# Recurrence of a hybrid trunk: keys of all batches projected first, front and inverse 0 beside the receptance projections, the value input mixed early and reread from DRAM

## The chip, the core and the metric

The program runs on one core of a Trainium2 chip. The core has a matrix engine (TensorE: PE, and PEld for its weight loads), a vector engine (VectorE, DVE), a scalar engine (ScalarE, ACT), a general engine (GpSimd, POOL), a synchronising engine that issues nearly all transfers (SyncE, SP), and 16 DMA engines. Tiles live in SBUF, matmul results in eight banks of PSUM. The metric is the device time of one execution in microseconds (us), as the median of several runs.

## The reference

Two layers over a sequence of 512 positions of width 1024, in fp32: layer 0 mixes tokens with an RWKV-7 recurrence, layer 1 with a chunked spatial gating unit, and a SwiGLU network (width 2816) follows each. The change touches only the recurrence:

```python
xx = _token_shift(x) - x
xs = x[None] + xx[None] * mix[:, None, None, :]
r, k, v = jnp.einsum('cbtd,cde->cbte', xs[:3], w_rkv)
w_raw = (w0 + jnp.tanh(xw @ w1) @ w2)
decay = jnp.exp(-jnp.exp(-softplus(-w_raw) - 0.5))
a = sigmoid(a0 + (xa @ a1) @ a2);  g = sigmoid(xg @ g1) @ g2
kk = normalised(k * k_k);  k = k * (1.0 + (a - 1.0) * k_a)
# per head, state S (64 x 64), t = 0..511:
#   S = S diag(decay_t) + (S (-kk_t)) (kk_t a_t)^T + v_t k_t^T ;  y_t = S r_t
y = groupnorm(y) * gn_w + gn_b + sum(r * k * r_k) * v
out = (y * g) @ w_o
```

Here `xs[0]`, `xs[1]` and `xs[2]` are the receptance, key and value inputs: each is the normed x and its shift by one position, mixed with its own coefficients.

## The kernel before

Every fp32 operand of a large matmul is split into a rounded part (hi, made by ACT) and a rest (lo, made by DVE), and three matmuls give the product (`mm3`). The kernel runs the recurrence, its output projection, network 0, the gating unit and network 1. The program is written in order into a tile framework; the pools give out slots by tag, and a planner at build time (`schedule_with_timeline_sim=True`) fixes each engine's order from a simulated course in which an instruction may pass earlier ones that are not ready or have no slot.

The 16 heads are handled in four batches of four heads. For each batch b:

- **P** (`kr_proj`, L654): the key and the receptance projection, each of two weights (`feat_proj`, L647): a weight of 512 KB is loaded by SP, split into whi and wlo (two buffers each, L182), and 24 matmuls of 512 columns go into one of two "pl" banks; ACT copies the result out (L660). The inputs are the mixed and split tiles xk and xr (`mixed_split`, L616): per tile ACT and DVE mix (L612, L613), then ACT and DVE split.
- **E** (`early`, L740): decay, its running sum and exponentials, key normalisation, bonus; it ends by storing four scaled arrays to DRAM (sa, sb: L811, L814).
- **F** (`front`, L824): loads them back (ST, L829; MV, L835), multiplies them chunk by chunk (lm, L851), and spreads the products into MV, BX and LA by ACT copies and POOL selections (L854 to L870).
- **B** (`back`, L873): inverts a unit triangular matrix per chunk: one DVE transposition (LX, L882), 15 dependent steps on DVE (L896, L898), two transpositions (L901, L902), chains of 32x32 matmuls on PE (Qp, Np, Tp, Q2p, T2p: L918 to L950) with copies into bdT, then products that close MV (mp, L959; gh, L966; L968, L969).
- **S** (`scan`, L971): eight dependent steps of small matmuls (us, L995; Yp, L1008) with the value rows reread from DRAM (L980), and the output Y.
- **N** (`finish`, L1077): group norm, bonus and gate, stored to DRAM (od) for the output projection; batch 3 is kept on chip in halves.

**X** mixes and splits the value input once for all batches, and **V** (`v_proj`, L698) projects the values of batch b (384 matmuls of 256 columns for all four, in two "pb" banks) and stores them to DRAM.

The order of the program is the list PLAN (L35): after the hidden layer of the gate and the mixing of xk come P0 (in which xr is mixed), E0, P1, E1, P2, E2, P3, E3, X0, F0, B0, F1, V0 to V3, B1, S0, F2, S1, F3, N0, B2, N1, B3, S2, N2, S3, N3. XV (L36) says in which pool each of the eight value tiles lies.

The slots matter to the change: "s" has 17 tiles of 4 KB a partition (h, half of xk, xr, part of the value input, MV, BX), "x" 4 (half of xk, part of the value input, then Y), "e2" 7 (k, r, Pp, ST, LA, LX and, later, split output weights), "e" 2 of half the size (xs, vev, ob), "f0", "gain" and "hn" 2 each, "bd" 1 (the tile tws of early 1 and 3, later bdT) and "hid" 1 (the hidden layer of decay, later Dt).

Of the kernel before, what the change touches and what calls it, by code (L numbers as in the profile page):

```python
# [13 lines left out]
P = 128  # L14
# [5 lines left out]
C = 64  # L20
# [11 lines left out]
BANKS_F1 = dict(tr=(1, 2), gu=(4, 0, 3, 5, 7, 6), R=(4, 0), Q=(3, 5), Z=(7, 6), h0=(1, 2, 0, 5), h1=(4, 3, 7, 6))  # L32
SLOTS = 17
E2 = 7
PLAN = "P0 E0 P1 E1 P2 E2 P3 E3 X0 F0 B0 F1 V0 V1 V2 V3 B1 S0 F2 S1 F3 N0 B2 N1 B3 S2 N2 S3 N3".split()  # L35
XV = "xxxessss"  # L36
XSLOTS = 13
LAG = 2
PLAIN = 2
# [91 lines left out]
class Trunk:  # L131
# [384 lines left out]
    def rwkv(self, x0):  # L516
# [3 lines left out]
        with ExitStack() as ctx:  # L520
# [4 lines left out]
            sa = [dp.tile([P, 2, NC, 2, C], F32, name="sa") for _ in range(4)]  # L525
            sb = [dp.tile([P, 2, NC, 2, C], F32, name="sb") for _ in range(4)]
            od = dp.tile([KT, P, T], F32, name="od")

            def e(name, shape=(P, T), dt=F32):
                return rp.tile(list(shape), dt, name=name, tag="e", bufs=2)  # L530
# [85 lines left out]
            def mixed_split(c, where):  # L616
# [6 lines left out]
                    r.append(s)  # L623
                return r

            wrkv = i["rwkv_w_rkv"][0]
            q2 = range(2)
            units = [(hh, q) for hh in range(2) for q in q2]
# [22 lines left out]
                    self.mm3(acc, (hi[:, kt, :], lo[:, kt, :]), (xs[kt][:, 0, :], xs[kt][:, 1, :]), kt == 0, kt == KT - 1)  # L651
                return acc

            def kr_proj(b):  # L654

                o = []
                for w, xs, n in ((wrkv[1], xk, "k"), (wrkv[0], xr, "r")):
                    t = e2(n)
                    for q in q2:
                        a.copy(t[:, q, :], feat_proj(w, xs, 2 * b + q))  # L660
                    o.append(t)
                return o

            sg = rp.tile([P, 2, T], F32R, name="sg")
            sgb = rp.tile([96, T], F32R, name="sgb")
# [74 lines left out]
            def early(b, k, r):  # L740
# [4 lines left out]
                fcs = lambda q: slice(q * P, (q + 1) * P)  # L745


                if b % 2:
                    tws = bd("tws", [P, 2, 2, T])
                    tw, ta = tws[:, 0], tws[:, 1]  # L750
                    room = lambda name: self.sm.tile([P, 2, T], F32, name=name, tag="hn", bufs=2)
                else:
                    tw, ta = (self.f0p.tile([P, 2, T], F32, name=n, tag="f0", bufs=2) for n in ("tw", "ta"))
                    room = lambda name: gslot(name, [P, 2, T])
# [69 lines left out]
            def front(b, o):  # L824

                MV, ST, BX = {}, {}, {}
                for hh in range(2):
                    st = ST[hh] = e2("ST", (P, 2, 4, 2, C))
                    nc.sync.dma_start(out=st.rearrange("p q c n t -> p q (c n t)"),  # L829
                                      in_=sb[b][:, :, 4 * hh:4 * hh + 4].rearrange("p q c n t -> p q (c n t)"))  # L830
                    for q in q2:
                        mv = MV[hh, q] = s4("MV", [P, 4, 2, 2, C])
                        for hd in range(2):
                            g.memset(mv[head[1 - hd], :, :, hd], 0.0)
                            nc.sync.dma_start(out=mv[head[hd], :, :, hd].rearrange("p c n t -> p (c n) t"),  # L835
                                              in_=sa[b][head[hd], q, 4 * hh:4 * hh + 4].rearrange("p c n t -> p (c n) t"))
                LA = e2("LA", (P, 2, NC, C))
                Dm = self.f0p.tile([P, 2, 528], F32, name="Dm", tag="f0", bufs=2)
                g.memset(full(Dm), 0.0)
                g.memset(Dm.rearrange("p b r -> p (b r)")[:, 0:1024:33], 1.0)  # L840
                for hh, q in units:
                    st, mv = ST[hh][:, q], MV[hh, q]

                    bx = BX[hh, q] = s4("BX", [P, 4, 4, C])
                    for hd in range(2):
                        g.tensor_copy(bx[head[hd], 2 + hd], self.ident[head[hd], head[hd]].unsqueeze(1).broadcast_to([64, 4, C]))
                    for hd in range(2):
                        rows, other = head[hd], head[1 - hd]
                        lm = self.bank("pl", "lm")
                        for cc in range(4):  # L850
                            mm(lm[:, cc * P:(cc + 1) * P], st[:, cc].rearrange("p n t -> p (n t)"), mv[:, cc, :, hd, :], start=True, stop=True)  # L851
                        lv = lm.rearrange("p (c a t) -> p c a t", c=4, a=2)
                        la = LA[:, q, 4 * hh:4 * hh + 4]
                        a.copy(mv[other, :, :, hd], lv[other])  # L854
                        for n in range(2):
                            upper(mv[other, :, n, hd], n - 1)
                        a.copy(la[rows], lv[rows, :, 0, :])
                        upper(la[rows], -1)
                        a.copy(bx[rows, 1], lv[rows, :, 1, :])
                        upper(bx[rows, 1], 0)  # L860

                    sf = st.rearrange("p c n t -> p c (n t)")
                    pt = self.bank("pl", "bkt")
                    for cc in range(4):
                        nc.tensor.transpose(pt[:, cc * P:(cc + 1) * P], sf[:, cc], self.ident)
                    pv = pt.rearrange("p (c h f) -> p c h f", c=4, h=2)
                    for hd in range(2):
                        rows, other = head[hd], head[1 - hd]
                        a.copy(bx[rows, 0], pv[rows, :, hd])
                        a.copy(bx[other, 2 + hd], pv[other, :, hd])  # L870
                o.update(MV=MV, BX=BX, LA=LA, Dm=Dm)

            def back(b, o):  # L873
# [18 lines left out]
                for j in range(15):  # L892
# [3 lines left out]
                    v.tensor_tensor(tv, LXd[:, :, j + 1:16, j:j + 1].broadcast_to([P, 2, n, j + 1]),  # L896
                                    Dmd[:, :, j:j + 1, 0:j + 1].broadcast_to([P, 2, n, j + 1]), op=ALU.mult)
                    v.tensor_tensor(Dmd[:, :, j + 1:16, 0:j + 1], Dmd[:, :, j + 1:16, 0:j + 1], tv, op=ALU.add)  # L898
                Dt = rp.tile([P, 16, 2, 32], F32, name="Dt", tag="hid", bufs=1)
                Dn = self.sm.tile([P, 16, 2, 32], F32, name="hn", tag="hn", bufs=2)  # L900
                v.transpose(Dn.rearrange("p u x s -> p s (u x)"), full(Dm).rearrange("p t s -> p s t"))  # L901
                v.transpose(Dt.rearrange("p u x t -> p t (u x)"), full(Dm))  # L902
# [68 lines left out]
            def scan(b, o, then=None):  # L971

                MV, pc = o["MV"], o["pc"]
                Y = xslot("Y", [P, TT, 2, P])

                def new_su(c):
                    su = rp.tile([P, 2, 2, C], F32, name="su", tag="su", bufs=4)
                    vv = Vd[c * C:(c + 1) * C, 2 * b * P:2 * b * P + 2 * P].rearrange("t (q h v) -> t q h v", q=2, h=2)
                    for hd in range(2):
                        nc.sync.dma_start(out=su[64 * (1 - hd):64 * (1 - hd) + 64, :, hd, :], in_=vv[:, :, hd, :])  # L980
                        if c == 0:
                            g.memset(su[64 * hd:64 * hd + 64, :, hd, :], 0.0)
                    return su

                su = new_su(0)
                for c in range(NC):
                    hh, cc = c // 4, c % 4
                    tt, par = c // 2, c % 2
                    if c < NC - 1:
                        nsu = new_su(c + 1)  # L990
                        us = self.bank("us", "us")
                        for q in q2:
                            for hd in range(2):
                                rows = slice(64 * hd, 64 * hd + 64)
                                mm(us[rows, q * C:(q + 1) * C], MV[hh, q][:, cc, 0, hd, :], su[:, q, hd, :], start=True, stop=True)  # L995

                        v.tensor_tensor(nsu[0:64, :, 0, :], us[0:64, 0:2 * C].rearrange("p (q v) -> p q v", q=2),
                                        pc[0:64, :, c:c + 1].broadcast_to([64, 2, C]), op=ALU.mult)
                        for q in q2:
                            a.activation(nsu[64:128, q, 1, :], us[64:128, q * C:(q + 1) * C], AF.Copy,  # L1000
                                         scale=pc[64:128, q, c:c + 1])
                    if par == 0:
                        yp = self.bank("yp", "Yp")
                    yr = slice(64 * par, 64 * par + 64)
                    for q in q2:
                        for hd in range(2):
                            yc = slice(q * P + hd * C, q * P + hd * C + C)
                            mm(yp[yr, yc], MV[hh, q][:, cc, 1, hd, :], su[:, q, hd, :], start=True, stop=True)  # L1008
                    if par == 1:
                        a.copy(Y[:, tt].rearrange("p q f -> p (q f)"), yp[:, 0:2 * P])  # L1010
                    if c < NC - 1:
                        su = nsu
                    if then and c == NC // 2 - 1:
                        then(Y)
                return Y
# [79 lines left out]
            xr, kr, ops, Y = None, {}, {}, {}  # L1095
            for n in PLAN:
                f, b = n[0], int(n[1])
                if f == "P":
                    if xr is None:
                        xr = mixed_split(0, "ssssssss")  # L1100
                    kr[b] = kr_proj(b)
                elif f == "E":
                    ops[b] = early(b, *kr[b])
                elif f == "X":
                    xs = mixed_split(2, XV)
                elif f == "V":
                    v_proj(xs, [b])
                elif f == "F":
# [162 lines left out]
```

## Time and profile before

| what | value |
|---|---|
| time, median of 3 runs | 1363.42 us (1361.05 to 1363.58) |
| the profiled execution | 1364.19 us, its span 1362.5 us |
| TensorE clock granted, mean | 0.975 of full speed |
| HBM read and written | 124.35 MB and 14.16 MB |

The page gives busy time by engine, the span in 40 slices, the DMA queues, the chain of work that ended last, and groups of instructions; further answers of the trace cut the span into stretches or list one line or one tile. A row of a group reads: line, engine, operation, tile written and tiles read, shapes, count, then busy time and mean duration, then idle time of the engine just before them and what ended it. A row of one line reads: count, then the shortest, median and longest duration in ns and the first and last start in us. TensorE rows overlap, because a matmul's record holds its whole passage through the array: the durations of neighbouring matmuls do not add up to time.

In the span before, the recurrence with its output projection takes about the first 477 us, and network 0 begins there.

### The profile page before, as it was taken

Reading aid. Unit: us, or ns where it says so; the run is one execution under the profiler, and the core shown is the slowest. Engines: PE = TensorE matmul, PEld = TensorE weight load, DVE = VectorE, ACT = ScalarE, POOL = GpSimd, SP = SyncE. Lnnn points to the kernel's source line nnn. Section 1 sums busy time; section 2 is a strip of 40 time slices with the busy share of each in tenths; the row PEclk is TensorE's granted clock in tenths of the full one; section 3 lists DMA queues with packets and bytes.
Section 4 is the critical chain, followed back from the end, with each engine's and each line's share of the span. In section 5 each row is a group of like instructions: output and inputs, shape, how many; then the busy total and the mean of one; then the engine's idle time right before and its main releaser. Section 6 shows DMA issues by size and latency. Waiting matters only on the chain. (4 is left out here: it accounts for less than half of the span.)

```text
span 1362.5 us, 24563 instructions
## 1 busy us (share of the span) xinstructions
PE 1289.8 (95%) x9812; PEld 1120.0 (82%) x9812; DVE 894.2 (66%) x1515; ACT 694.9 (51%) x1240; POOL 193.2 (14%) x311
## 2 busy tenths in 40 slices
PE   5989999989789989999999999999989999999998
PEld 3657789878677787999998887878878999998886
DVE  7875676477837499778785325575479787786223
ACT  7975795576333364455454314543364554464221
POOL 1000184575100024000000002010122000000000
PEclk9989999899799988999999999999989999999999
DMA  5136595322214233343323232242322433323321
GB/s 157 38 89 154 138 221 162 108 73 78 78 42 153 63 105 90 112 117 100 106 78 109 93 116 86 79 151 80 108 82 72 126 109 94 109 63 117 99 94 62
DMA packets 217266, 140.10 MB, mean 103 GB/s; under 512 B 67856, under 2 KB 193344, under 8 KB 217152
## 3 DMA queue, kind: packets, MB, share of 16 engines
q1 hardware_dynamic: 215856, 133.81, 34.0%
q0 software_dynamic: 1296, 4.72, 1.0%
q8 instruction: 77, 1.26, 0.4%
q14 instruction: 37, 0.30, 0.1%
HBM read 124.35 MB, written 14.16 MB: 102 GB/s over the span
## 5 line engine op out<-in xcount | busy, mean ns | idle before, releaser
L180 DVE TENSOR_TENSOR wlo<-wraw,whi 128x1024 fp32r<-128x1024 f32 x105 | 129.6, 1234 | 195.2 <-ACT whi L179 187.4
L179 ACT CAST whi<-wraw 128x1024 fp32r<-128x1024 f32 x105 | 110.0, 1048 | 227.9 <-PE acc L204 136.5
L204 PE MATMUL acc<-whi,actw 128*128 128x512 f32 x704 | 220.7, 394 | 0.0
L204 PEld LDWEIGHTS acc<-whi,actw 128*128 128x128 f32 x704 | 132.3, 188 | 30.6
L204 PE MATMUL Q<-bc,whi 128*128 128x256 f32 x864 | 156.3, 281 | 1.1 <-ACT hn L421 1.1
L204 PE MATMUL acc<-wlo,actw 128*128 128x512 f32 x352 | 138.7, 394 | 0.0
L204 PEld LDWEIGHTS Q<-bc,whi 128*128 128x128 f32 x864 | 133.4, 189 | 1.5 <-ACT hn L421 1.3
L179 ACT CAST whi<-wsum 128x1024 fp32r<-128x1024 f32 x72 | 75.5, 1051 | 101.1 <-DVE wsum L377 35.5
L204 PE MATMUL Q<-bc,wlo 128*128 128x256 f32 x432 | 121.5, 281 | 0.0
L204 PE MATMUL Z<-bc,whi 128*128 128x256 f32 x576 | 107.9, 285 | 3.3 <-ACT whi L179 3.3
L204 PE MATMUL R<-bc,whi 128*128 128x256 f32 x576 | 108.1, 285 | 0.9 <-ACT Q L392 0.9
L180 DVE TENSOR_TENSOR wlo<-wsum,whi 128x1024 fp32r<-128x1024 f32 x72 | 86.7, 1221 | 18.9 <-ACT whi L179 18.9
L204 PE MATMUL gu<-hT,whi 128*128 128x256 f32 (+1 forms) x384 | 92.2, 334 | 3.6 <-DVE hT L62 3.4
L204 PEld LDWEIGHTS Z<-bc,whi 128*128 128x128 f32 x576 | 90.6, 192 | 4.2 <-ACT whi L179 4.2
L204 PEld LDWEIGHTS R<-bc,whi 128*128 128x128 f32 x576 | 91.0, 192 | 1.3 <-ACT Q L392 1.1
L204 PE MATMUL proj<-xsp,whi 128*128 128x512 f32 x256 | 85.2, 411 | 5.7 <-ACT xsp L179 3.1
L179 ACT CAST whi<-wq 128x1024 fp32r<-128x1024 f32 x54 | 56.7, 1049 | 58.1 <-issue 18.4
L180 DVE TENSOR_TENSOR wlo<-wq,whi 128x1024 fp32r<-128x1024 f32 x54 | 65.9, 1222 | 30.9 <-ACT whi L179 30.8
L204 PE MATMUL Z<-bc,wlo 128*128 128x256 f32 x288 | 81.9, 284 | 0.0
L204 PE MATMUL R<-bc,wlo 128*128 128x256 f32 x288 | 81.9, 284 | 0.0
L204 PEld LDWEIGHTS Q<-bc,wlo 128*128 128x128 f32 x432 | 81.9, 189 | 0.0
L204 PEld LDWEIGHTS acc<-wlo,actw 128*128 128x128 f32 x352 | 66.1, 188 | 15.3
(346 smaller groups left out, 2883.3 us busy)
## 6 DMA issues: line engine op xcount, KB each, us to landing
wraw<-in_ffn_w_down_dram SPq DMA_DIRECT2D x44, 512.0 KB, 3.7
wq<-in_ffn_w_gate_dram SPq DMA_DIRECT2D x72, 256.0 KB, 3.0
wq<-in_ffn_w_up_dram SPq DMA_DIRECT2D x72, 256.0 KB, 3.5
wraw<-in_rwkv_w_rkv_dram SPq DMA_DIRECT2D x24, 512.0 KB, 4.9
wraw<-in_sgu_w_in_dram SPq DMA_DIRECT2D x16, 512.0 KB, 4.2
x<-in_x_dram SPq DMA_DIRECT2D x8, 512.0 KB, 4.2
ST<-sb SPq DMA_DIRECT2D x8, 512.0 KB, 6.2
MV<-sa SPq DMA_DIRECT2D x32, 128.0 KB, 3.8
```

The lines of the kernel that those rows point to most:

```text
L179: self.nc.scalar.copy(hi, src)
L180: self.nc.vector.tensor_tensor(lo, src, hi.bitcast(F32), op=ALU.subtract)
L204: self.nc.tensor.matmul(out, l, r, start=start, stop=stop, skip_group_check=resumed)
```

## The change

The list PLAN is rewritten, P is split into K (key) and R (receptance), and M is new. K0, R0 and E0 still come first; then K1, M0, K2, K3; then F0, R1, E1, B0, R2, E2, R3, E3; then X0, F1, V0, V1, B1, S0, V2, V3, F2, S1, B2, N0, F3, N1, B3, S2, N2, S3, N3. M mixes the value input and stores it, unsplit, to a new DRAM tile xvd (8 stores of 256 KB); X rereads it (8 loads through "e" tiles) and splits it. With this go moves between pools: two value tiles lie in e2 and six in "s"; k of batch 3 lies in "s"; tw, ta and cum of early 2 and 3 lie in "s" instead of "f0", "gain" and "bd"; BX of batches 0 and 2 lies in the x slots; Dt of inverse 0 lies in "s"; Y lies in e2 instead of x. Sizes of pools, tiles and arithmetic stay.

```diff
-PLAN = "P0 E0 P1 E1 P2 E2 P3 E3 X0 F0 B0 F1 V0 V1 V2 V3 B1 S0 F2 S1 F3 N0 B2 N1 B3 S2 N2 S3 N3".split()
-XV = "xxxessss"
+PLAN = "K0 R0 E0 K1 M0 K2 K3 F0 R1 E1 B0 R2 E2 R3 E3 X0 F1 V0 V1 B1 S0 V2 V3 F2 S1 B2 N0 F3 N1 B3 S2 N2 S3 N3".split()
+XV = "eessssss"
...
+            xvd = dp.tile([KT, P, T], F32, name="xvd")
...
+            def reread_split(where):
+                r = []
+                for kt in range(KT):
+                    t = e("xs")
+                    nc.sync.dma_start(out=t, in_=xvd[kt])
+                    s = dict(s=s4, e=e2)[where[kt]]("xsp", [P, 2, T], F32R)
+                    self.split(s[:, 0, :], s[:, 1, :], t)
+                    r.append(s)
+                return r
...
-            def kr_proj(b):
-
-                o = []
-                for w, xs, n in ((wrkv[1], xk, "k"), (wrkv[0], xr, "r")):
-                    t = e2(n)
-                    for q in q2:
-                        a.copy(t[:, q, :], feat_proj(w, xs, 2 * b + q))
-                    o.append(t)
-                return o
+            def kr_proj(b, w, xs, n):
+
+                t = (s4 if n == "k" and b == 3 else e2)(n, (P, 2, T))
+                for q in q2:
+                    a.copy(t[:, q, :], feat_proj(w, xs, 2 * b + q))
+                return t
...
-                if b % 2:
+                if b >= 2:
+                    tw, ta = (s4(n, [P, 2, T]) for n in ("tw", "ta"))
+                    room = lambda name: s4(name, [P, 2, T]) if name == "cum" else self.sm.tile([P, 2, T], F32, name=name, tag="hn", bufs=2)
+                elif b % 2:
...
-                    bx = BX[hh, q] = s4("BX", [P, 4, 4, C])
+                    bx = BX[hh, q] = (s4 if b % 2 else xslot)("BX", [P, 4, 4, C], F32)
...
-                Dt = rp.tile([P, 16, 2, 32], F32, name="Dt", tag="hid", bufs=1)
+                Dt = rp.tile([P, 16, 2, 32], F32, name="Dt", tag="hid", bufs=1) if b else s4("Dt", [P, 16, 2, 32])
...
-                Y = xslot("Y", [P, TT, 2, P])
+                Y = e2("Y", (P, TT, 2, P))
...
-                if f == "P":
+                if f == "K":
+                    kr["k", b] = kr_proj(b, wrkv[1], xk, "k")
+                elif f == "R":
                     if xr is None:
                         xr = mixed_split(0, "ssssssss")
-                    kr[b] = kr_proj(b)
+                    kr["r", b] = kr_proj(b, wrkv[0], xr, "r")
+                elif f == "M":
+                    for kt in range(KT):
+                        nc.sync.dma_start(out=xvd[kt], in_=mixed(2, kt))
                 elif f == "E":
-                    ops[b] = early(b, *kr[b])
+                    ops[b] = early(b, kr["k", b], kr["r", b])
                 elif f == "X":
-                    xs = mixed_split(2, XV)
+                    xs = reread_split(XV)
```

## The prediction

> **What bounds the kernel now.** I read the page first, for the engine that fills the span.
>
> ```profile
> span 1362.5 us, 24563 instructions
> PE 1289.8 (95%) x9812; PEld 1120.0 (82%) x9812; DVE 894.2 (66%) x1515; ACT 694.9 (51%) x1240; POOL 193.2 (14%) x311
> PE 21%; DVE 0%; ACT 0%; DVEq 0%; issue 0%
> ```
>
> TensorE is busy 95% of the span, and the chain that ended last holds almost only PE, but it reaches back no further than the second feed-forward network. So the chain says nothing of the recurrence, where the change lies. For that I cut the trace into stretches.
>
> ```profile
> core 0: us, PE busy (x) PEld busy (x) DVE busy (x) ACT busy (x) POOL busy (x), PEclk, DMA share, GB/s
> 60.00:90.00 30.00, 24.18 (x77) 14.54 (x78) 20.15 (x28) 25.45 (x38) 0.00 (x0) 0.89 0.14 40
> 90.00:160.00 70.00, 70.00 (x341) 52.50 (x340) 40.16 (x46) 44.43 (x58) 0.13 (x1) 1.00 0.60 153
> 160.00:180.00 20.00, 20.00 (x138) 16.14 (x137) 18.98 (x24) 16.00 (x26) 14.74 (x23) 1.00 0.86 215
> 180.00:230.00 50.00, 46.87 (x422) 46.20 (x421) 32.43 (x50) 37.42 (x76) 32.45 (x61) 1.00 0.81 200
> 340.00:370.00 30.00, 21.03 (x302) 17.23 (x300) 27.14 (x68) 11.18 (x17) 4.52 (x8) 0.77 0.24 80
> 414.00:477.00 63.00, 57.73 (x324) 44.39 (x322) 38.18 (x109) 22.14 (x55) 2.38 (x1) 0.97 0.35 108
> 230.00:414.00 184.00, 163.51 (x2969) 142.28 (x2969) 115.15 (x269) 101.14 (x241) 69.39 (x159) 0.93 0.27 76
> ```
>
> Columns: stretch, its length, busy us of each engine, granted clock, DMA share. The reader is to see three regimes. From 90 to 160 (key and receptance projections) PE is full and POOL idle. From 160 to 230 (fronts beside value projections) PE is nearly full and everything else is loaded, the DMA at over 0.8. From 230 to 414 PE lacks 184.00 - 163.51 = 20.5 us and its clock falls to 0.93; the deepest hole is 340 to 370, with 9 us idle, a clock of 0.77, and DVE at 27.14 of 30.
>
> What sets the pace there is the chain of each head batch: front, inverse (opened on DVE by one transposition LX), closing products, scan.
>
> ```profile
> L882 DVE STREAM_TRANSPOSE LX<-LA x4: 1930/1963/2040, 213.2 to 337.7; 128x1024 f32<-128x1024 f32 x4
> L1008 PE MATMUL Yp<-su,MV x256: 222/222/356, 259.0 to 431.7; 128*64 128x64 f32 x128
> L204 PE MATMUL v<-whi,xsp x256: 274/283/682, 170.6 to 251.9; 128*128 128x256 f32 x128
> POOL BX L846 <- PE v L204: 14.0, 3, 10.1
> L851 PE MATMUL lm<-MV,ST x256: 270/275/582, 183.0 to 333.4; 128*128 128x128 f32 x128
> 179.03 0.40 PE L204 MATMUL v<-whi,xsp 128*128 128x256 f32 x2
> 179.38 0.40 PE L204 MATMUL v<-whi,xsp 128*128 128x256 f32 x2
> 342.10 1.24 PE L941 MATMUL Q2p<-Dn,LA 32*32 32x32 f32 x62
> 353.93 1.92 PE L950 MATMUL T2p<-bdT,Q 32*32 32x32 f32 x64
> ```
>
> The first and the last of the four LX start at 213.2 and 337.7: a batch every (337.7 - 213.2) / 3 = 41.5 us. The last scan matmul starts at 431.7. The dense value matmuls (v) are used up at 251.9, when only the first inverse is near its end. So three and a half chains run on without dense work to fill PE. The waits row shows one brake: POOL waited three times, 10.1 us at the longest, for value matmuls before it could write the next BX tile, that is for a slot that their input held.
>
> **The change part by part.**
>
> *Start to 90 us.* Receptance 0 still stands second, so its inputs are mixed at the same place:
>
> ```profile
> 80.90 0.73 PE L204 MATMUL proj<-xsp,whi 128*128 128x512 f32 x2 [3.08 <-ACT xsp L179]
> 83.82 0.80 PE L204 MATMUL proj<-xsp,whi 128*128 128x512 f32 x1 [2.18 <-DVE xsp L180]
> ```
>
> PE waits 3.08 + 2.18 us here for that mixing. Key 1 could fill the hole only if its split weights had room; whi and wlo have two buffers each, and receptance 0, first in the program, holds both. I take 0, between -5 (hole filled) and +4 (the new mixing gets between).
>
> *Value mixing early, and its round trip.* The eight mixings of the value input move from beside receptance 3 to behind key 1; nothing is saved.
>
> ```profile
> L612 ACT ACTIVATE xs<-h,omix x32: 707/722/769, 21.5 to 176.2; 128x512 f32<-128x512 f32 x32
> L613 DVE SCALAR_TENSOR_TENSOR xs<-h,vecT,xs x32: 732/751/880, 23.3 to 177.0; 128x512 f32<-128x512 f32 x32
> L179 ACT CAST xsp<-xs x24: 601/619/625, 39.6 to 179.9; 128x512 fp32r<-128x512 f32 x24
> L180 DVE TENSOR_TENSOR xsp<-xs,xsp x24: 679/692/819, 40.4 to 180.5; 128x512 fp32r<-128x512 f32 x24
> od<-ob SPq DMA_DIRECT2D x6, 256.0 KB, 2.0
> wq<-in_ffn_w_up_dram SPq DMA_DIRECT2D x72, 256.0 KB, 3.5
> MV<-sa SPq DMA_DIRECT2D x32, 128.0 KB, 3.8
> L835 SPq DMA_DIRECT2D MV<-sa x32: 573/632/1763, 177.2 to 313.2; - x32
> L660 ACT COPY k<-proj x8: 571/578/589, 62.6 to 159.8; 128x512 f32<-128x512 f32 x8
> ```
>
> ACT does 8 x 0.722 = 5.8 us and DVE 8 x 0.751 = 6.0 us at about 90 to 110, where in 90 to 160 they have 26 and 30 us free. New are 8 stores and 8 loads of 256 KB. The store has the shape of od (2.0 us to landing), the load is nearest to the 256 KB weight load (3.5 us); on SP 16 issues at 0.632 = 10 us, spread over some 100 us. SP's queue runs in order: behind a store that waits for its mixing stand weight loads, and PE waits for those. Eight key weights, with as many of the receptance between them, are copied out from 62.6 to 159.8: one weight in about 6.5 us, with a second buffer loaded ahead. So I take 0; bounds 0 and +8.
>
> At the value input's end the loads pass through two "e" tiles: four pairs of 3.5 + 0.619 + 0.692 = 4.8 us, 19 us in all. The first pair can wait ready (two tiles lie in e2), the other six need slots that the receptance input frees only in its last projection, whereas before half of the input lay in tiles the key input had freed already. The first half-weight of the values can start after two pairs, 9.6 us, of which front 1 and late parts of early 3 cover about half. I take +4, between 0 and +11.
>
> *Front and inverse 0 forward.* They now lie beside receptance 1 to 3. Their ACT, DVE and POOL work goes into a stretch where POOL is idle and ACT and DVE are about 60% used; the same matmuls run, so PE has as much to do. The early parts of batches 1 to 3 slip, but theirs isn't the last wait before front 1. What is late next is front 1: in slots of tag "s" it meets MV of batch 0 (4), the value input (6), its own MV (4) and BX (4): 18 of 17. BX 0 lies in x slots now, but the last BX of front 1 still waits for scan 0 or the last value matmul.
>
> What it is worth: one of the four chains leaves the thin stretch and dense work (receptance 1 to 3, then values 2 and 3 behind scan 0) covers the next. By the chain alone up to one batch period, 41.5 us, would go. By PE, no more than it lacks: 20.5 us of busy time from 230 to 414. I take -20, the PE bound, since the holes are what the moved work can fill; ends 0 and -41.5.
>
> The Trainium skill, "Perfetto Trace Analysis", section "Identifying the Most-Contended Engine", says that matmul busy share does not show how far TensorE is from its limit and that the LDWEIGHTS busy share does. By that rule the room here is 184.00 - 142.28 = 41.7 us and the sum below would come to -18 - 21 = about -39. The row cannot decide between the two; the second rival below ends at the same place by the chain.
>
> *Inverse 2 ahead of the norm of batch 0.* Before, N0 stands ahead of B2; in the new order behind it. From the start of Q2p (342.10) to that of T2p (353.93) inverse 2 took 11.8 us while DVE, 27.14 of 30 us busy, worked on norm 0, inverse 3 and copies alike. Norm 0 then moves, and its DVE time is not saved: I take -4; ends -10 and 0.
>
> *Tiles.* The scan's Y goes into e2 (7 tiles), where ST, LA and LX of the next fronts also live, and three pairs of split output weights. Front 3 needs four of the seven while Y of two batches may live: +2, between 0 and +8. The tail is left as it is: from 414 to 477 PE is busy 57.73 of 63 us, and this stretch moves with the scan.
>
> **Sum:** 0 + 0 + 4 - 20 - 4 + 2 = -18 us. The profiled execution took 1364.19 us (span 1362.5 and 1.7 around it), 0.8 above the median of 1363.42 (three runs, 1361.05 to 1363.58). 1364.19 - 18 = **1346**.
>
> **The rivals.**
>
> ```profile
> L1008 PE MATMUL Yp<-su,MV x64: 222/222/270, 259.0 to 289.8; 128*64 128x64 f32 x64
> ```
>
> *Slots close the chain again (slower).* The row is scan 0 alone: 30.8 us, ending at 289.8. Place: the last BX of front 1, which waits for the slots that scan 0 gives back. While it waits, lm of that unit keeps both "pl" banks, and the transpositions that inverse 1 and front 2 need go through the same banks; so scan 0, inverse 1 and front 2 run one after another. It decides if scan 0, waiting for the late value input, begins at 259 or later as before: then nothing of the chain is early, and the slots cost on top. Price: the -20 becomes 0, the X stretch its +11, e2 +5, N0's move -4: +12, so 1376. For it: 18 of 17, and the 10.1 us wait of the same kind. Against: scan 0 needs only the values of batch 0; three of their matmuls take 0.35 us (179.03 to 179.38 above), so the 96 of one batch 11 us. DMA crowding leads to the same side: the share is 0.60 to 0.86 while 4 MB are added.
>
> *The chain alone leads (faster by more).* The holes close, the clock is back at 1.00, and a whole batch period goes: 0 + 0 + 4 - 41.5 - 4 + 2 = -39.5, so 1325. For it: clock 0.93 over 184 us. Against: the 2969 matmuls there, most of them small, wait on each other.
>
> *The order doesn't take hold (no change).* The engines work out of program order already: front 0's lm runs from 183.0 on between value matmuls (170.6 on) that stand behind it. If front 0 finds no free slots until the key input is gone and the planner lets the rest slip to where it was, the end stays within 3 us: 1363.
>
> **How the numbers follow.** Forecast 0.50, own range 1331 to 1359 (the chain term at -35; or at -12 with 5 more for X and e2); larger gain 0.16; no change 0.07; slower 0.27. Faster by over 0.2% (2.7 us, about what a measurement of this kernel can tell from no change): 0.50 + 0.16 = 0.66; within: 0.07; slower: 0.27. The range takes in most of both rivals: from 1318, where under 0.1 is left, to 1378, where about 0.1 is left.
>
> **What would show it.** Right: the first LX before 160 and the last before 315; the last Yp before 415; v matmuls still running beside scan 0; 340 to 370 with PE over 25 of 30. The X term: a PE gap of some us at the first v matmul, ended by a DMA or a split of xsp. The tile term: a POOL wait for BX or a DMA wait for ST ended by Y's last reader. It is wrong if the first LX comes early and the last one stays near 338 (the slot rival), if PE waits for wraw between 90 and 200 (the DMA), or if the time after the last Yp grows beyond 45 us, the gain being given back in the output projection.

## The result, and the profile after

The changed kernel took 1404.02 us (median of four runs, 1401.88 to 1406.06). Run beside it, the kernel before took 1363.5. The ratio is 1.0302, 95% interval 1.0269 to 1.0334: slower by 3%, 41 us, where 18 us less had been forecast. Lines have moved: LX is now at L893, Yp at L1019, ST at L840, Y at L1021, BX at L857; the tanh that opens the work of `early` on ACT is at L769.

The page of the changed kernel:

```profile
span 1404.4 us, 24587 instructions
PE 1306.8 (93%) x9812; PEld 1133.5 (81%) x9812; DVE 895.8 (64%) x1515; ACT 694.3 (49%) x1240; POOL 174.8 (12%) x311
```

The same 9812 matmuls fill 1306.8 us instead of 1289.8, and the rest of the span grows from 1362.5 - 1289.8 = 72.7 to 97.6. So of the 41.9 us, 24.9 are idle time of TensorE and 17.0 are busy time: matmuls that ran slower or overlapped less, which the page doesn't tell apart. The stretches say where; they are those of the prediction, now of the changed kernel:

```profile
core 0: us, PE busy (x) PEld busy (x) DVE busy (x) ACT busy (x) POOL busy (x), PEclk, DMA share, GB/s
90.00:160.00 70.00, 65.01 (x363) 50.66 (x362) 34.05 (x44) 45.47 (x80) 27.11 (x63) 1.00 0.69 177
160.00:180.00 20.00, 20.00 (x208) 15.61 (x207) 14.62 (x30) 5.12 (x7) 1.17 (x3) 1.00 0.50 129
180.00:230.00 50.00, 41.26 (x472) 32.14 (x470) 16.90 (x31) 19.37 (x30) 3.16 (x8) 0.66 0.10 34
340.00:370.00 30.00, 27.96 (x549) 25.99 (x549) 21.55 (x50) 15.64 (x33) 10.22 (x22) 1.00 0.57 164
414.00:477.00 63.00, 50.30 (x751) 40.95 (x750) 37.62 (x82) 20.45 (x42) 0.74 (x1) 0.78 0.31 94
230.00:414.00 184.00, 163.09 (x2181) 147.19 (x2181) 116.58 (x238) 113.54 (x251) 74.19 (x168) 0.91 0.49 133
```

The reader is to see the third stretch. From 180 to 230 every engine is short of work at once: DVE falls from 32.43 to 16.90 us, ACT from 37.42 to 19.37, POOL from 32.45 to 3.16, the DMA share from 0.81 to 0.10, and TensorE is granted 0.66 of its clock where it had 1.00. That is no full resource; something stands behind something else. The old hole at 340 to 370 is indeed filled (27.96 of 30), and the lack from 230 to 414 is what it was (20.9 against 20.5 us), but 2181 matmuls are done there instead of 2969: all of it lies later.

The chain of each batch, by line and by tile:

```profile
L893 DVE STREAM_TRANSPOSE LX<-LA x4: 1908/1958/2092, 143.2 to 401.6; 128x1024 f32<-128x1024 f32 x4
L1019 PE MATMUL Yp<-su,MV x256: 222/222/369, 277.6 to 484.2; 128*64 128x64 f32 x128
L204 PE MATMUL v<-whi,xsp x256: 274/282/686, 188.8 to 355.3; 128*128 128x256 f32 x128
```

Inverse 0 begins 70 us earlier (143.2 for 213.2), but the first scan 18.6 us later (277.6 for 259.0); the last inverse begins 64 us later, and the last matmul of the last scan 52.5 us later. The value matmuls start 18 us late and then last until 355.3, not 251.9. The timeline of the stretch shows what they stood behind (TensorE's and ACT's rows):

```profile
197.09 1.71 PE L977 MATMUL gh<-BX,MVt 64*128 64x128 f32 x16 [0.68 <-ACT MVt L972]
...
212.95 3.10 PE L977 MATMUL gh<-BX,MVt 64*128 64x128 f32 x16 [0.68 <-ACT MVt L972]
215.96 1.19 PE L204 MATMUL w<-hid,wa2h 64*128 64x512 f32 x2
...
217.61 0.69 ACT L769 ACTIVATE tw<-w,halfb 128x512 f32<-128x512 f32 x1 [4.72 <-PE w L204]
...
233.85 0.58 PE L204 MATMUL v<-whi,xsp 128*128 128x256 f32 x1 [4.90 <-ACT xsp L179]
```

The first matmul of early 2 (w, at 215.96) starts just as the last product of inverse 0 (gh) ends, and the values resume only 18 us after that. It needs no result of inverse 0: it waited for a PSUM bank, as e2 below shows. In the program, early 2 draws its results from banks 0, 7, 3 and 4 in turn, inverse 0 works in 3 and 4, and early 2 is written behind inverse 0. In the built program (the one that the planner made of this order) the first w lies in bank 3 and waits for the DVE additions that read the gh of inverse 0 there.

From early 2 the delay went on to front 1. This is POOL's row where it first writes MV tiles of front 1:

```profile
242.75 1.09 POOL L845 MEMSET MV<- 64x512 f32 x2 [25.34 <-DMA sa<-tw]
```

POOL had nothing to do for 25 us until the store of early 2's tw gave its slot back. In the built program the four MV tiles of front 1 take the slots that tw, ta and cum of early 2 and ta of early 3 leave, all of them tiles that the change had moved into "s".

### The profile page after: what moved, and what is told of

It is laid out like the page before. It is cut to its first block, busy times and chain, and to the rows that moved or that the text cites. A ratio compares the mean times of both kernels' runs of the same rounds, so it can differ in the third digit from the quotient of the medians.

```text
span 1404.4 us, 24587 instructions
## 1 busy us (share of the span) xinstructions
PE 1306.8 (93%) x9812; PEld 1133.5 (81%) x9812; DVE 895.8 (64%) x1515; ACT 694.3 (49%) x1240; POOL 174.8 (12%) x311
```

## The experiments

The first theory, the **queue theory**: a tile is given a slot or bank of its tag in the order of the program, so what is written later waits for what is written earlier even if its data are there. Rivals: the round trip through DRAM costs the time (transfer theory), or front 0's work on ACT, DVE and POOL delays what lay there (load theory). Ratios are to the kernel before, run beside it on the same chip; 0.001 is 1.4 us. The intervals reach 0.002 to 0.006 to each side, so a difference of two ratios is known to between 4 and 9 us.

### One piece at a time

**e1**, the kernel before with the early mixing and the reread alone:

```diff
-PLAN = "P0 E0 P1 E1 P2 E2 P3 E3 X0 ..."
+PLAN = "P0 E0 P1 M0 E1 P2 E2 P3 E3 X0 ..."
...
-                    xs = mixed_split(2, XV)
+                    xs = reread_split(XV)
```

> The kernel before with one part of the change alone: the value input is mixed early (behind P1), stored to DRAM and reread; order, pools and all else as before. Transfer theory (the round trip through DRAM and its two tiles delays the values): 15 to 40 us slower than before, with the first value matmul well behind 171. Queue theory (tiles of one tag, slots and banks, are given out in program order, and early 2 stands behind inverse 0): the round trip costs little, within 4 us of the kernel before.

Measured 1371.28 us, 1.0041 (1.0022 to 1.0059): +5.6 us. The transfer theory falls as main cause. The value input lies in its old slots here.

**e2**, the changed kernel with early 2 and 3 on banks of their own:

```diff
-                    acc = self.bank("pe", "w")
+                    acc = self.bank("pe2" if b >= 2 else "pe", "w")   # pe2=(0, 7); likewise a, ssp, bps
```

> The changed kernel, but early 2 and 3 take their matmul results in banks 0 and 7 alone, not in 3 and 4, which inverse 0 uses ahead of them. Queue theory: the first tanh of early 2 moves from 217.6 to between 170 and 185 (next in its way is Dt of inverse 0, the tile ahead of it in tag s, written at 171), the bulk of the value matmuls begins before 210 instead of 234, and the time falls by 15 to 35 us, to 1369 to 1389. Transfer theory: values stay past 230, time 1400 to 1408. Load theory (front and inverse 0 beside the early parts overload ACT, DVE and POOL): early 2 begins sooner but all runs slower, 1396 to 1408.

Measured 1387.51 us, 1.0151 (1.0115 to 1.0186): by the ratios 0.0151, or 20.6 us, less than the changed kernel (known to 7 us; the medians, from two chips, differ by 16.5). Rows of its timeline (start, duration, engine, line), then its row for the stretch from 180 to 230:

```profile
171.47 1.27 ACT L769 ACTIVATE tw<-w,halfb 128x512 f32<-128x512 f32 x2
...
218.40 0.58 PE L204 MATMUL v<-whi,xsp 128*128 128x256 f32 x1
```

```profile
180.00:230.00 50.00, 44.62 (x537) 36.72 (x536) 30.37 (x46) 31.49 (x47) 6.72 (x12) 0.76 0.51 135
```

Early 2 comes 46 us earlier, the value matmuls resume 15 us earlier, DVE has 30.37 us of work in the stretch instead of 16.90. Front 1 comes sooner with it: its MV tiles are first written at 224.31 and LX of inverse 1 starts at 267.88, where the changed kernel has 242.75 and 285.32. The bank was the block, and the load theory, which asked for 1396 or more, falls; that the values would resume before 210 was wrong by 8 us.

**e3** (values 2 and 3 written ahead of inverse 1 and scan 0) and **e4** (front 0 and its transpositions on banks 5 and 6 instead of those of the projections):

```diff
-F1 V0 V1 B1 S0 V2 V3 F2
+F1 V0 V1 V2 V3 B1 S0 F2
...
-                        lm = self.bank("pl", "lm")
+                        lm = self.bank("pl" if b else "pb", "lm")   # likewise bkt, mvt
```

> The changed kernel with values 2 and 3 ahead of inverse 1 and scan 0 in the program. Queue theory: their bank 5 is no longer behind the closing products of inverse 1, the value input gives its six slots back by 300 instead of 356, the last LX comes before 380 instead of at 401.6, and the time falls by 8 to 25 us, to 1379 to 1396. Transfer and load theory: the order of the last two values matters little, 1400 to 1408.

> The changed kernel with front 0 and the first transpositions of inverse 0 in the value banks 5 and 6 instead of the two banks that the projections use. Queue theory: receptance 1 runs between the matmuls of front 0, so PE loses less from 126 to 155; but early 2 still waits for inverse 0, so most of it is lost again: 0 to 8 us faster, 1396 to 1404. Load theory: no change, 1402 to 1406, and front 0 itself not quicker.

Measured 1407.27 (1.0299, 1.0265 to 1.0333) and 1405.99 (1.0287, 1.0243 to 1.0331): nothing from either, a miss for e3, and in e4 what the load theory gave (1402 to 1406). e4 does fill TensorE from 120 to 160 (40.00 us busy for 35.01), but starts inverse 0 20 us later (163.6) and gains nothing by it. e3 did what it was to do, and to no use; its rows by line:

```profile
L893 DVE STREAM_TRANSPOSE LX<-LA x4: 1926/2016/2077, 143.3 to 377.4; 128x1024 f32<-128x1024 f32 x4
L1019 PE MATMUL Yp<-su,MV x256: 222/222/366, 281.2 to 473.3; 128*64 128x64 f32 x128
```

The last inverse begins 24 us sooner and the last scan ends 11 us sooner, yet the span is 1403.2 us, 1.2 less than that of the changed kernel: the stages behind the scan gave it back. Why, these runs don't settle.

### Order or storage

The next four split the change in two: its storage (which tile lies in which pool, and the reread) and its order. **e5** has the edits of e2, e3 and e4 together; **e6** the changed order with inverse 0 behind the value input; **e7** the new storage with the order of the kernel before; **e8** the same with the keys first.

```diff
e6 +K0 R0 E0 K1 M0 K2 K3 F0 R1 E1 R2 E2 R3 E3 X0 B0 F1 V0 V1 B1 S0 V2 V3 F2 S1 B2 N0 F3 N1 B3 S2 N2 S3 N3
e7 +K0 R0 E0 K1 R1 M0 E1 K2 R2 E2 K3 R3 E3 X0 F0 B0 F1 V0 V1 V2 V3 B1 S0 F2 S1 F3 N0 B2 N1 B3 S2 N2 S3 N3
e8 +K0 R0 E0 K1 M0 K2 K3 R1 E1 R2 E2 R3 E3 X0 F0 B0 F1 V0 V1 V2 V3 B1 S0 F2 S1 F3 N0 B2 N1 B3 S2 N2 S3 N3
```

> The changed kernel with all three edits that were tried singly: early 2 and 3 on banks 0 and 7, the values of batches 2 and 3 ahead of inverse 1, front 0 and its transposes on banks 5 and 6. One at a time they gave -16.5, +3 and +2 us. Queue theory: with early 2 free of inverse 0's banks the two other queues become the ones that end last, so the three together gain more than the first alone: 1362 to 1382 us, value matmuls done in one stretch before 275, inverse 1's LX before 265. If they only add: 1386 to 1394. Load theory (the earlier front's own work on ACT, DVE and POOL is what delays the rest): 1386 or more.

> The changed kernel with inverse 0 behind early 2, early 3 and the value input in the program; front 0 stays early, keys stay first. Queue theory: nothing of early 2, early 3 and the value input stands behind inverse 0 in any queue of banks or slots, so early 2's tanh comes before 185, the value matmuls begin before 215, and the time is 1368 to 1388 us. Load theory: front 0 and its sixteen-step solve are as early as before, so 1397 to 1411.

> The changed kernel's storage (tiles of early 2 and 3, key 3 and Dt in other slots, Y in a pair, value input through DRAM) with the order of the kernel before: keys and receptance of a batch together, front 0 and inverse 0 behind the value input, norm 0 ahead of inverse 2. Queue theory: the order made the loss, the storage did not, so what is left is the round trip (measured at +5.5) and a few us: 1364 to 1378 us. Storage theory (the moved tiles themselves are the loss): 1385 to 1405.

> The same storage, with the keys of all batches projected first but front 0, inverse 0, norm 0 and inverse 2 where the kernel before has them. Queue theory: keys first puts nothing behind inverse 0, so it adds at most 6 us to the run with the old order: 1364 to 1384 us. Theory that the keys themselves are to blame (receptance 1, and with it early 1, 2 and 3, come some 30 us later, and the value input behind them): 1388 to 1408.

| run | us | ratio (95%) |
|---|---|---|
| e5 | 1390.44 | 1.0200 (1.0150 to 1.0249) |
| e6 | 1394.50 | 1.0234 (1.0176 to 1.0292) |
| e7 | 1394.06 | 1.0225 (1.0174 to 1.0277) |
| e8 | 1398.90 | 1.0257 (1.0208 to 1.0306) |

All four miss what the queue theory expected, and e7 is the one that turned it: with the order of the kernel before, the new storage alone loses 0.0225 of the 0.0302. The order as a whole adds 0.0077. (e8 lies 4.8 us above e7, which is within the noise of the two.) The queues had been looked for in the wrong half.

### Which tile

In e7 front 2 stood still until scan 0 had begun to write its output Y (ST goes out at 284.00, Y's first write starts at 282.64), which had been moved into the pairs ("e2") among ST, LA and LX. **e11** moves only Y, on top of e1; **e12** is e7 with Y back in the x slots (and so BX 0 and 2 back in "s"); **e13** the changed kernel with the same two put back; **e9** is the kernel before with the late part of the new order alone (inverse 2 ahead of norm 0 and of front 3).

```diff
e11
-                Y = xslot("Y", [P, TT, 2, P])
+                Y = e2("Y", (P, TT, 2, P))
e12, e13
-                    bx = BX[hh, q] = (s4 if b % 2 else xslot)("BX", [P, 4, 4, C], F32)
+                    bx = BX[hh, q] = s4("BX", [P, 4, 4, C])
-                Y = e2("Y", (P, TT, 2, P))
+                Y = xslot("Y", [P, TT, 2, P])
e9
-S0 F2 S1 F3 N0 B2 N1 B3
+S0 F2 S1 B2 N0 F3 N1 B3
```

> The kernel before with the reread through DRAM (first run of the study, +5.5 us) and one thing more: Y, the scan's output, takes one of the seven pairs that the state tiles (ST), LA and LX of the inverses take too, instead of one of four x slots. Pair theory: a front's ST loads wait for the pair that Y of an earlier scan holds (in the run with the old order and the new storage front 2's ST landed at 284, in the first run at 262), and this is the loss of the old order's run: 1383 to 1402 us, front 2's ST after 278. BX theory (the loss of that run comes from BX 0 and 2 in the x slots, or from tw, ta, cum, key 3 and Dt in the s slots, none of which is here): 1366 to 1378 us. The prediction's +2 for this step gives about 1371.

> The run with the old order and the new storage, with Y back in the x slots and with it BX 0 and 2 back in the s slots; tw, ta, cum, key 3 and Dt stay in the s slots. Pair theory: 1362 to 1378 us, as the kernel before with the reread. Theory of the s slots (the early tiles there are the loss): 1385 to 1400.

> The changed kernel, order and all, with Y back in the x slots and BX 0 and 2 back in the s slots. Pair theory: the loss that Y makes goes, that of the order (early 2 and the values behind inverse 0) stays: 1374 to 1392 us. If the order alone makes the loss of the changed kernel: 1396 to 1412. The prediction's slots rival (18 tiles for 17 s slots) would make it slower than the changed kernel: above 1408.

> The kernel before with one part of the change alone: inverse 2 ahead of norm 0, front 3 ahead of norm 1 (the order S1 B2 N0 F3 N1 B3). The prediction's term for it was -4, between -10 and 0: 1353 to 1364 us. Rival: norm 0 holds its Y, and DVE work of inverse 2 stands ahead of it, so the output of scan 0 comes back later and the end moves by as much: 1365 to 1372 us.

| run | us | ratio (95%) |
|---|---|---|
| e11 | 1389.75 | 1.0207 (1.0181 to 1.0234) |
| e12 | 1383.42 | 1.0155 (1.0133 to 1.0177) |
| e13 | 1420.94 | 1.0420 (1.0379 to 1.0462) |
| e9 | 1361.78 | 0.9991 (0.9975 to 1.0008) |

One line, Y's pool, costs 1.0207 - 1.0041 = 0.0166, 22.6 us, where the prediction had +2. First the kernel with the reread alone, then the one with Y moved too (SP's and ACT's rows of the timeline, ST being the load of front 2, and below the dots the row of the line of LX):

```profile
261.74 1.21 SPq L840 DMA_DIRECT2D ST<-sb  x2
...
L893 DVE STREAM_TRANSPOSE LX<-LA x4: 1958/1964/2064, 222.4 to 344.8; 128x1024 f32<-128x1024 f32 x4
```

```profile
277.95 0.37 ACT L1021 COPY Y<-Yp 128x256 f32<-128x256 f32 x1 [3.19 <-PE Yp L1019]
279.26 1.26 SPq L840 DMA_DIRECT2D ST<-sb  x2
...
L893 DVE STREAM_TRANSPOSE LX<-LA x4: 1890/1964/2057, 223.2 to 356.1; 128x1024 f32<-128x1024 f32 x4
```

ST goes out 17.5 us later, 1.3 us after the first write of Y, and the last LX starts 11 us later. e12 lands between the two theories: putting Y and BX back wins 0.0070 (10 us, known to 8), and the tiles left in the s slots (those of early 2 and 3, key 3, Dt and six of the value input) still cost 1.0155 - 1.0041 = 0.0114 (15.5 us). These runs don't take those tiles apart, but the trace of e12 names one wait among them, that of POOL for the store of early 3's tw, before it could write the last BX of front 0:

```profile
194.87 1.93 POOL L857 COPY BX<-ident 64x256 f32<-64x256 f32 x2 [16.62 <-DMA sa<-tw]
```

In e1 all eight of these copies were done by 179.0, and the first LX starts at 222.4 there and at 229.0 in e12. e13 shows the mechanism of the prediction's slots rival, one front later: with BX 0 and 2 in the s slots the changed order loses another 16 us, and the last BX of front 2, at 350.86, is written behind value matmuls. e9 shows that the late reordering alone changes nothing that can be measured in the kernel before.

### Do the causes add, and is it room or order

**e18** is the changed kernel with Y in the x slots, BX 0 there too (they are free again before scan 0) and BX 2 in "s"; **e16** adds the banks of e2; **e17** adds e3 and e4 as well; **e15** is e7 with eight pairs and sixteen s slots in place of seven and seventeen.

```diff
e18, e16, e17
-                    bx = BX[hh, q] = (s4 if b % 2 else xslot)("BX", [P, 4, 4, C], F32)
+                    bx = BX[hh, q] = (s4 if b else xslot)("BX", [P, 4, 4, C], F32)
-                Y = e2("Y", (P, TT, 2, P))
+                Y = xslot("Y", [P, TT, 2, P])
e15
-SLOTS = 17
-E2 = 7
+SLOTS = 16
+E2 = 8
```

> The changed kernel with its order, Y back in the x slots and BX 2 back in the s slots; BX 0 stays in the x slots, which it gives back before the first scan. Pair theory (Y in the pairs cost 18 to 23 us in the kernel before): the changed kernel less that, 1378 to 1390 us, with front 2's ST before 285. Order theory (early 2 and the values behind inverse 0 are the whole loss, and the pairs do not end last in this order): 1397 to 1411.

> The same, with early 2 and 3 on banks 0 and 7 besides (that alone gave -16.5 us). If the two causes add: 1361 to 1375 us. If they overlap, each hiding the other: 1376 to 1388.

> The same again, with the values of batches 2 and 3 ahead of inverse 1 and front 0 on banks 5 and 6, which alone and beside the first gave nothing. With the pairs free, the values in one stretch give back the value input's slots early, so front 2 and 3 come sooner: 1352 to 1370 us by the queue theory; as much as the run before it (within 5 us) if the slots were not what held front 3.

> The run with the old order and the new storage, Y still in a pair, with eight pairs in place of seven and sixteen s slots in place of seventeen. Pair theory (it is the number of pairs, not which memory Y lies in): 1366 to 1382 us, front 2's ST before 272. If Y in the pairs costs by another way (its address, its readers): 1388 to 1400.

| run | us | ratio (95%) |
|---|---|---|
| e18 | 1425.04 | 1.0448 (1.0405 to 1.0491) |
| e16 | 1404.42 | 1.0307 (1.0261 to 1.0352) |
| e17 | 1378.32 | 1.0110 (1.0071 to 1.0149) |
| e15 | 1390.00 | 1.0197 (1.0150 to 1.0244) |

None of the four lands where the pair or queue theory put it, e17 by 8 us; together they show why edits made singly gave little. In the changed order the value input keeps its s slots until its last matmul, so BX 2, moved into "s" to make place for Y, comes late; a row of POOL's timeline in e18, and the row of the value matmuls as one tile:

```profile
350.44 0.83 POOL L857 COPY BX<-ident 64x256 f32<-64x256 f32 x2 [0.21 <-PE v L204]
...
L204 PE MATMUL v<-whi,xsp x240: 274/282/681, 234.1 to 357.2; 128*128 128x256 f32 x120
```

One queue is opened and the next one closes. The early banks still win 0.0141 there (e18 to e16), as they did with Y in a pair (0.0151), so what they win doesn't hang on where Y lies. But the values first together with e4's banks, worth nothing from e2 to e5, are worth 0.0197, 27 us, once Y is out of the pairs (e16 to e17). Part of that is the wait of BX 2 for the value input, which the edit of e18 had made itself. The step from e5 to e17, which changes only where Y and BX 2 lie, wins 0.0090, 12 us (known to 9). In e17 the last inverse and the last scan are where the changed kernel had them 39 and 32 us later:

```profile
L204 PE MATMUL v<-whi,xsp x256: 274/281/682, 177.9 to 287.9; 128*128 128x256 f32 x128
...
L893 DVE STREAM_TRANSPOSE LX<-LA x4: 1961/1984/2090, 163.0 to 362.5; 128x1024 f32<-128x1024 f32 x4
...
L1019 PE MATMUL Yp<-su,MV x256: 222/222/314, 261.0 to 452.2; 128*64 128x64 f32 x128
```

e17 is the best of the changed orders and still 1.1% slower than the kernel before. From 180 to 230 TensorE is busy for 40.90 of 50 us in it, no more than in the changed kernel; what holds it there, no run here takes up.

An eighth pair (e15) left ST where it was, so room is not the point (timeline, and below the dots the value matmuls):

```profile
281.01 0.37 ACT L1021 COPY Y<-Yp 128x256 f32<-128x256 f32 x1 [2.48 <-PE Yp L1019]
282.32 1.26 SPq L840 DMA_DIRECT2D ST<-sb  x2
...
L204 PE MATMUL v<-whi,xsp x256: 274/280/683, 171.8 to 259.4; 128*128 128x256 f32 x128
```

By the addresses of that program, the pair that front 2's first ST was given had held a tile of the value input, and the last value matmul starts at 259.4: it stood free for more than 20 us. The load itself waits for no engine in the built program, only for an older load to land and for its turn in SP's queue. That turn was given by the plan: 16 instructions behind the first write of Y, and behind value rows of scan 0. In e1, where Y lies elsewhere, the load goes out at 261.74. So what should hold ST is its place behind Y among the pairs, when the plan is made. **e20** (on e11) and **e22** (on e5) change nothing but that place, for fronts 2 and 3:

```diff
+            def state(b, hh):
+                st = e2("ST", (P, 2, 4, 2, C))
+                nc.sync.dma_start(out=st..., in_=sb[b]...)
+                return st
...
                 elif f == "S":
+                    for hh in range(2 if b < 2 else 0):
+                        early_st[b + 2, hh] = state(b + 2, hh)
```

> The kernel before with the reread and Y in the pairs, and only the order in which pairs are asked for changed: the two ST tiles of front 2 are taken and loaded in the program ahead of scan 0 (those of front 3 ahead of scan 1), so ahead of the Y of that scan. Still seven pairs, Y still in one. Order theory (a tile stands behind every earlier tile of its tag until that one has been given, even when a slot is free: in five runs front 2's ST landed about 1 us after scan 0's first write of Y, at eight pairs too): ST of front 2 before 272 instead of 280, its LX before 322 instead of 330, and 1366 to 1380 us instead of 1390. Number theory (seven pairs are too few with Y among them): 1386 to 1396.

> The changed kernel with the three edits of the fifth run (1390 us) and the same change of order: ST of fronts 2 and 3 taken ahead of scans 0 and 1, Y still in the pairs. Order theory: as much as with Y in the x slots (1378): 1371 to 1384 us, front 2's ST before 270. Number theory: 1386 to 1396.

Measured 1382.51 us, 1.0152 (1.0120 to 1.0184), for e20, and 1387.69 us, 1.0192 (1.0153 to 1.0232), for e22. In the timeline of e20 ST (now L839) no longer waits for Y, and LX (now L899) still starts beside the next Y:

```profile
269.93 1.28 SPq L839 DMA_DIRECT2D ST<-sb  x2
...
322.07 0.37 ACT L1027 COPY Y<-Yp 128x256 f32<-128x256 f32 x1 [0.26 <-PE Yp L1025]
...
322.34 1.93 DVE L899 STREAM_TRANSPOSE LX<-LA 128x1024 f32<-128x1024 f32 x1
```

So the order theory holds for ST of front 2: 279.26 in e11, 269.93 here, still 8 us behind e1 (in both built programs it stands right behind the LX of inverse 1, which is written ahead of it in the pairs). ST of front 3 goes out at 284.43 instead of 326.33, and the last LX starts 9 of its 11 us sooner (347.1). All this is worth about 0.0055 (7.5 us, known to 6) of Y's 0.0166; the time forecast for it missed by 2.5 us. In e22 ST of front 2 goes out 15 us sooner than in e5 (263.52 for 278.60), and yet nothing was won that can be told from e5: there the load isn't what front 2 waits for last. The time is the one that the number theory gave, and eight pairs were tried in the old order alone. LX of front 2, still written behind the next Y, starts beside Y's first write in e20, but in e22 it starts 0.5 us ahead of it. Its place in the built program (8 instructions behind that write) would fit the same cause, but no run moves LX alone, so for LX it is not shown. What makes the other 15 us of Y in a pair stays open.

## Why the prediction was wrong

Set against the kernel before, the loss parts as follows, by differences of the ratios: the reread 5.6 us (known to 2.5); the rest of the new storage, in the old order, 25.1 (e7 less e1, known to 8); the new order 10.5 (the changed kernel less e7, known to 8). Sum 41.2.

- **Start to 90 us, 0.** Nothing in these runs speaks against it (from 60 to 90 TensorE is busy for 23.34 us, before for 24.18).
- **Round trip 0, reread +4.** Measured together at +5.6 (3.0 to 8.0) with the value input in its old slots: within both ranges. The reason given for the +4, six slots that come free late, isn't in e1; it is a part of the 15.5 us below.
- **Front and inverse 0 forward, -20.** Wrong in sign. The step said that "the early parts of batches 1 to 3 slip, but theirs isn't the last wait before front 1". It was: early 2 slipped behind inverse 0, because of two PSUM banks that the step never listed, and the value input, front 1 and scan 0 came behind early 2. Front 1 waited for it by way of the moved tiles, whose slots its MV tiles take (the 25.34 us above). The block by the banks is worth 0.0151, 20.6 us. With it gone (e2) the new order wins 0.0074 (10 us, known to 9) over the old one on the same storage (e7), keys first and the late reordering included: a gain of about half of what was put down, covered twice over by the block. The new order on the old storage was not tried.
- **Inverse 2 ahead of norm 0, -4.** e9: -1.2, between -3.4 and +1.1. The end of the range that lay at nothing was the right one.
- **Tiles, +2 (0 to +8).** The mis-sized term: Y in a pair costs 22.6 us by itself in the old order. The step counted how many pairs are needed, and that would have been enough room; it did not ask which tile is written before which. The moves of the early tiles, key 3 and Dt into the s slots were given no price at all; together with the value input's six slots they cost 15.5 us where BX lies there too.
- **LDWEIGHTS share, -39.** The Trainium skill's rule ("Perfetto Trace Analysis", section "Identifying the Most-Contended Engine") was weighed there with a room of 41.7 us. After the change the same stretch still has 184.00 - 147.19 = 36.8 us of it, in a kernel that is 41 us slower: the row did not tell whether this change could use it.
- **The slots rival, 1376.** Its condition came true (scan 0 from 277.6, later than 259) and its side was right. Its place was so only in part. The last BX of front 1 does come late, at 290.61, and in the built program it takes the slot of an MV tile that scan 0 gives back; but LX of inverse 1 had already started at 285.32. What front 1 had waited for before that was early 2 and 3. e13 and e18 show the rival's mechanism where BX 0 and 2, or 2 alone, go back to "s". Its price took the gain away; no rival made the moved work itself a block.
- **What would show it.** First LX before 160: yes. Last LX before 315: 401.6. Last Yp before 415: 484.2. PE over 25 of 30 from 340 to 370: yes, and worthless as a sign, since other work had slipped into the stretch. After the last Yp no more than before: so the loss lies in the recurrence, as said.

## What to carry to other kernels

Before work is moved forward in a program that is planned ahead, list for each tag of slots and banks which tiles are then written in front of which: a moved tile can delay those that stand behind it in its tag, even with a slot free, as ST shows. Counting slots is not enough, and a hole that fills proves nothing; look for the stretch where all engines lack work at once. Where several such queues follow one another, a fix can look worthless alone (e3, and e5 beside e2) and win beside another one (e17), so try them together too, and see that the other fix hasn't made a new wait which the first then takes away.

## What the runs showed of the hardware

**The lost clock.** 17 of the 41.9 us are not idle time but busy time, and a part of it is the clock. The sixteen gh matmuls of one unit took 1.71 us at 197, where the granted clock was 0.96 (197 to 200), and 3.10 us at 213, where it was 0.50 (200 to 216), although TensorE counts as busy for 13.97 of those 16 us. So the block, a chain of small matmuls with nothing dense beside it, also lengthened itself. The Trainium skill ("TensorE: Matmul & The Clock Gate", section "What's actually happening") says that the clock is let through in part by default and released by activity; the two speeds agree, with a factor of 3.10 / 1.71 = 1.8. Which kind of activity is too little, these rows don't tell.

**More banks, less overlap.** The Trainium skill ("Perfetto Trace Analysis", section "Matmuls") advises that independent groups of matmuls rotate through different banks. Here the rotation over four banks was what tied early 2 to inverse 0; over the two of them that inverse 0 does not use, the kernel was faster by 0.0151 of the ratio, about 20 us. What a rotation wins here hangs on who else holds the banks at that time.
